# Hymba decoder layer on one core: per-row-block norm and block sums in the second feed-forward, residual in DRAM between the output-projection halves, one weight pool, five plain openers

## The chip, the cores and the metric

The kernel runs on one NeuronCore of a Trainium2 chip. TensorE (PE) multiplies matrices into PSUM; VectorE (DVE), ScalarE (ACT) and GpSimd (POOL) work on tiles in SBUF; SyncE (SP) issues most of the DMA transfers and POOL issues some. Each engine carries out its own list of instructions in order and waits on semaphores of the others. The metric is the device time of one launch in microseconds, lower is better.

## What is computed

One decoder layer on 1024 tokens of width 1024 with 16 meta tokens in front: a half-weighted SwiGLU feed-forward, a mixer of two head groups with an output projection, and a second half-weighted SwiGLU feed-forward, each behind an RMS norm and with a residual.

```python
h = h + 0.5 * swiglu(rms_norm(h, ffn1_norm[l]), ffn1_w_in[l], ffn1_w_out[l])
u = rms_norm(h, mix_norm[l]) @ w_in[l]
...
o_hg = hgrn2(hq, hf, hi, hg, lb_all[l], hgrn_out_norm[l], valid)
o_sb = stick_breaking(sq, sk, sv, sb_q_norm[l], sb_k_norm[l], valid)
o = jnp.concatenate([o_hg, o_sb], axis=-1).astype(h.dtype)
h = h + o @ w_out[l]
h = h + 0.5 * swiglu(rms_norm(h, ffn2_norm[l]), ffn2_w_in[l], ffn2_w_out[l])
```

swiglu(h) is (silu(h @ w_gate) * (h @ w_up)) @ w_out with a hidden width of 2816. Everything is float32.

## The kernel before

**Products in three matmuls.** Each float32 operand is split in two float32r halves: ACT casts to a high half ("wh", "xh", "th", lines 147, 221, 252, 270, 510), then DVE subtracts it to leave a low half ("wl", "xl", "tl", lines 149, 222, 253, 272, 512). A product is three matmuls, high by high, low by high, high by low. So each block of weights or activations costs PE nothing until ACT and DVE have split it.

**Feed-forwards by a seven-product scheme.** The feed-forward matrices are cut two by two and multiplied with seven products in place of eight (Strassen-Winograd): the data blocks B11, B21, B12, B22 give the operands B11, B21, T2, T3, T1, T4, B22, where T2, T3, T1 and T4 are sums of blocks. POOL forms the sums of weight blocks (line 285), DVE those of the data. `fast_in` (from line 257) does the input side: for each pair of column blocks f, one `quad` for the gate and one for the up half. A `quad` takes seven weight operands in turn, 12 matmuls each; PSUM banks a, b and c hold partial sums, which DVE adds up (lines 355, 411, 420). `wp` holds three rotating buffers each for wh, wl and for POOL's sums s, and `in_bufs` buffers for raw weights as they arrive.

The first feed-forward handles 272 of its 1040 rows plainly and 2 x 384 rows by the scheme. Its first four column pairs are "openers": their plain parts (`plain_quad`, four operands each for gate and up, 12 matmuls of 272 columns for each operand) run ahead of everything else, while the remaining rows are loaded, normed (`norm_rows`), transposed on PE eight at a time (`turned`, `first_block`) and combined (`first_combined`, 20 pieces of one cast and one or more subtractions). Each call of `next(steps)` runs one `plain_quad`; four pieces stand between two of them. For later pairs the plain part shares the operands of the quad (`also`), with one more operand; for openers the quad runs alone.

The second feed-forward (n = 512, all rows by the scheme) has two pairs as openers: of their four quads, the B11 and B21 products run first, as the T operands are not there yet.

**`fast_out`** (from line 483) does the output side: seven passes of 11 steps q, each with a weight block `left` (raw loads into `ring`, or the kept tiles sk and ak) and an activation block `right` from DRAM; `between(step, q)` is a hook. In the first feed-forward the hook carries the norm of the plain rows (`first_norm`): squares, `inv_rms_rows` in bank x0, `spread_rows` in x1, then four groups of transposes "hb" that all use bank y3.

**Between the feed-forwards** the output projection runs in two halves over k. The first half (`first_half_of_o`, 16 blocks (i, b) of column half i and row block b, 12 matmuls each, "wo<-wh,oT") is woven between the last recurrence steps of the HGRN heads. At the end of each block it loads the residual `res` and DVE writes the sum into hN2, a tile of 32 KB per partition that stays in SBUF. The second half ("wo<-wh,oH", pool `wo2`, its eight weight blocks of w_out split when it starts) adds to hN2 row block by row block; after each row block `normed(b)` writes the row to DRAM (h2N), norms it (`row_norm`, lines 236 to 240), transposes it (line 247) into the tile `whole`, and for b < 4 splits it into B11 and B21. After the last row block `fast_in` starts; `blocks()` (lines 1684 to 1696) then forms the sums with 16 subtractions of 128x512 and splits 20 tiles of 128x512 (`halve`).

**What sets the order.** PE's order is the program's (manual_schedule). On the other engines and on SP the planner puts in order what is ready, by program order or ahead of it inside `high_priority()`. Pools are stacked from the left or the right end of SBUF. A tile placed where an older pool's tiles were waits for the last use of those it overlaps (reuse_waits="tile").

Of the kernel before, what the change touches and what calls it, by code (L numbers as in the profile page):

```python
# [20 lines left out]
P = 128  # L21
D = 1024
# [17 lines left out]
class Block:  # L40
# [214 lines left out]
    def fast_in(self, ops, n, w_in, actD, openers, ev0, open_ev, feed=None, plain=None,  # L255
# [19 lines left out]
        def block(i, h, col):  # L275
            t = wp.tile([P, 4, P], F32, tag="raw", name="raw", bufs=self.in_bufs)
# [119 lines left out]
        def pair(f, opened=None, also=(None, None)):  # L396
# [17 lines left out]
            def up(i, j, ps, plus):  # L414
# [37 lines left out]
        if plain:  # L452
            for f in ahead:
                gate, up = plain_pair(f)
                plain_quad(f * P, gate)
                yield
                plain_quad(D_FF + f * P, up)
                yield
# [23 lines left out]
    def fast_out(self, out_of, n, w_out, actD, load_h, ready, between=lambda a, q: None,  # L482
# [5 lines left out]
        op, ring, pout = self.op, self.ring, self.pout  # L488
        nq = D_FF // 256
        nb = n // P  # L490
        sk = op.tile([P, nq, 512], F32, name="sk")
        ak = op.tile([P, nq, 512], F32, name="ak")
# [24 lines left out]
        def left(step, q):  # L517

            s, a = sk[:, q, :], ak[:, q, :]
# [16 lines left out]
            return raw(0, 1, q) if step == "A12" else raw(1, 1, q)  # L536
# [32 lines left out]
        for bank, a, b, start, (i, j) in steps:  # L569
# [4 lines left out]
            for q in range(nq):  # L574
                wh, wl = halved(left(a, q), "w", 512)
                xh, xl = halved(right((q, b), n), "t", n)
# [42 lines left out]
    def turned(self, rows, n, banks, evict):  # L619
# [3 lines left out]
        for k0 in range(0, KT, len(banks)):  # L623
            ks = range(k0, k0 + len(banks))
            ps = {k: self.pin.tile([P, n], F32, tag="q" + banks[k - k0], name="xps", bufs=2)
                  for k in ks}
# [6 lines left out]
            for k in ks:  # L633
                evict(k, ps[k])

# [17 lines left out]
    def first_plain(self, rows, junk, x):  # L653
# [9 lines left out]
        self.turned(rows, THIRDS[0][1], "ddbbccaa", evict)  # L663

    def first_block(self, ci, rows, pool, name, ops):
# [3 lines left out]
        got = []  # L669
# [8 lines left out]
        self.turned(rows, n, "bcbc", evict)  # L678
        return got
# [536 lines left out]
    def mix_out(self, k0, plan, o, hN, h1N, pool):  # L1216
# [3 lines left out]
        ws = {}  # L1220

        def part(i, b, k, kept):
            if k == 0:
                if i not in ws:
                    ws[i] = self.mix_weights(k0, i)
                kept["o"] = o(b)
                kept["ps"] = self.pproj.tile([P, 512], F32, tag="proj", name="wo")
# [5 lines left out]
            if k == 3:  # L1233
                h = hN[:, b, 512 * i : 512 * i + 512]
                if k0:
# [526 lines left out]
```

## Time and profile before

| | |
|---|---|
| time, median of 3 runs | 2117.18 us (2116.65 to 2118.34) |
| the profiled execution's own time | 2121.03 us |
| its span, first to last instruction | 2119.2 us |
| mean granted TensorE clock | 0.989 |
| DMA | 303.39 MB, mean 143 GB/s |

The profile's page gives busy time by engine. Its other views, asked of the same execution, are used below: the windows view (for each stretch of time the busy time of each engine with its number of instructions, the granted PE clock, the DMA share and rate), the waits view (who waited for whom: total, times, longest), the groups by line (count, busy time and mean duration in ns, then idle time before them), the chain of work that ended last, the timeline, and the DMA issues with their time to landing. In a row of the timeline stand the start, the duration, engine, line, operation, tiles and in brackets the idle time before it with what ended it. Of successive matmuls, the distance of their starts tells the rate, as their durations overlap.

### The profile page before, as it was taken

The page shows a single profiled execution, that of the slowest core. Times are in us where ns is not written, and L with a number is a line of the kernel's source. Part 1 is how long each engine was busy: PE and PEld are TensorE (multiplying, and loading weights), DVE is VectorE, ACT ScalarE, POOL GpSimd, SP SyncE. Part 2 cuts the span into 40 slices and gives each one's busy share as a digit, 9 for nine tenths or more (in the row PEclk, how much of TensorE's full clock was granted, in tenths as well). Part 3 has the DMA queues.
Part 4 walks back from the last instruction along what each step waited for, and adds up shares of the span by engine and source line. Part 5 has one row for each costly group of instructions (what it writes and reads, how often), then busy time and mean ns, then how long its engine had stood idle before and what let it go on. Part 6 is the DMA issues. An engine that isn't in the chain of part 4 may idle for free.

```text
span 2119.2 us, 31494 instructions
## 1 busy us (share of the span) xinstructions
PE 2028.9 (96%) x11249; PEld 1795.3 (85%) x11249; DVE 1373.6 (65%) x2067; ACT 902.8 (43%) x1854; POOL 624.8 (29%) x676
## 2 busy tenths in 40 slices
PE   7999999999999999999999999988899999999999
PEld 6999999999978799988888888866688888878887
DVE  6776545556688832367778686546667667666774
ACT  7533333334555534466666524145233323333443
POOL 2365534542000002253333201001445445440000
PEclk9999999999999999999999999989999999999999
DMA  6643222227865636343544144623233333349563
GB/s 201 190 142 104 97 82 96 98 67 256 280 213 172 207 108 201 128 138 110 136 121 115 65 179 125 179 90 124 83 107 105 97 108 106 99 158 313 189 224 114
DMA packets 280875, 303.39 MB, mean 143 GB/s; under 512 B 23504, under 2 KB 211280, under 8 KB 280720
## 3 DMA queue, kind: packets, MB, share of 16 engines
q1 hardware_dynamic: 264816, 253.48, 38.8%
q0 software_dynamic: 14864, 47.90, 5.9%
q8 instruction: 89, 1.46, 0.3%
q14 instruction: 66, 0.54, 0.1%
q10 hardware_dynamic: 1040, 0.00, 0.0%
HBM read 221.28 MB, written 80.04 MB: 142 GB/s over the span
## 4 chain that ended last, share of the span: by engine, by line
PE 80%; DVE 6%; DMA 2%; ACT 2%; issue 2%; POOL 0%; DVEq 0%; SPq 0%; ACTq 0%; POOLq 0%
PE o L582 15%; PE qb L313 14%; PE qc L313 9%; PE qa L313 9%; PE proj L162 5%; PE proj L164 5%; PE proj L163 5%; PE qd L313 4%; PE wo L1232 4%; PE o L548 3%; PE flip L1051 2%; PE lvl L820 2%; DMA raw<-in_ffn_w_out_dram 1%; DVE keep L1197 1%; PE oacc L1121 1%
## 5 line engine op out<-in xcount | busy, mean ns | idle before, releaser
L313 PE MATMUL qb<-T,wh 128*128 128x384 f32 (+1 forms) x1056 | 320.4, 364 | 5.8 <-DVE u L355 5.8
L272 DVE TENSOR_TENSOR wl<-s,wh 128x512 fp32r<-128x512 f32 x176 | 199.2, 1133 | 98.8 <-ACT wh L270 94.5
L313 PEld LDWEIGHTS qb<-T,wh 128*128 128x128 f32 x1056 | 196.5, 188 | 30.7 <-ACT wh L270 7.8
L313 PE MATMUL qa<-B,wh 128*128 128x384 f32 (+1 forms) x704 | 217.4, 371 | 3.6 <-ACT wh L270 3.6
L582 PE MATMUL o<-wl,th 128*128 128x512 f32 x539 | 210.4, 392 | 4.2 <-DVE wl L512 4.2
L582 PE MATMUL o<-wh,tl 128*128 128x512 f32 x539 | 210.0, 391 | 3.5 <-DVE tl L512 3.5
L582 PE MATMUL o<-wh,th 128*128 128x512 f32 x539 | 210.5, 392 | 0.0
L272 DVE TENSOR_TENSOR wl<-raw,wh 128x512 fp32r<-128x512 f32 x178 | 165.0, 930 | 63.7 <-ACT wh L270 60.3
L270 ACT CAST wh<-s 128x512 fp32r<-128x512 f32 x176 | 109.4, 622 | 225.8 <-PE qb L313 177.1
L162 PE MATMUL proj<-xh,wh 128*128 128x384 f32 (+2 forms) x576 | 205.4, 357 | 0.2 <-ACT xh L252 0.2
L163 PE MATMUL proj<-xh,wl 128*128 128x384 f32 (+2 forms) x576 | 199.6, 346 | 0.0
L164 PE MATMUL proj<-xl,wh 128*128 128x384 f32 (+2 forms) x576 | 199.2, 346 | 0.1
L313 PE MATMUL qb<-T,wl 128*128 128x384 f32 (+1 forms) x528 | 192.7, 365 | 6.6 <-DVE wl L272 6.6
L270 ACT CAST wh<-raw 128x512 fp32r<-128x512 f32 x178 | 109.8, 620 | 204.0 <-PE qc L313 104.9
L510 ACT CAST th<-act 128x512 fp32r<-128x512 f32 (+2 forms) x176 | 96.5, 549 | 190.8 <-PE o L582 140.3
L313 PEld LDWEIGHTS qa<-B,wh 128*128 128x128 f32 x704 | 132.7, 191 | 20.5 <-ACT wh L270 4.1
L512 DVE TENSOR_TENSOR tl<-act,th 128x512 fp32r<-128x512 f32 (+2 forms) x176 | 107.8, 616 | 63.1 <-ACT th L510 62.1
L313 PE MATMUL qd<-X,wh 128*128 128x272 f32 x704 | 146.1, 294 | 1.3 <-DVE X L661 0.9
L285 POOL TENSOR_TENSOR s<-raw 128x512 f32<-128x512 f32 x88 | 119.5, 1358 | 78.7 <-DVE wl L272 69.3
L313 PE MATMUL qa<-B,wl 128*128 128x384 f32 (+1 forms) x352 | 130.9, 372 | 5.0 <-DVE wl L272 5.0
L1197 DVE TENSOR_TENSOR_SCAN keep<-keep 128x144 f32<-128x144 f32 (+6 forms) x112 | 126.9, 1136 | 9.7 <-ACT keep L1193 7.4
L1202 POOL TENSOR_TENSOR sig<-sig,keep 128x144 f32<-128x144 f32 (+3 forms) x64 | 88.2, 1379 | 143.1 <-DVE keep L1197 80.0
(337 smaller groups left out, 4771.7 us busy)
## 6 DMA issues: line engine op xcount, KB each, us to landing
raw<-in_ffn_w_in_dram SPq DMA_DIRECT2D x216, 256.0 KB, 2.9
raw<-in_ffn_w_out_dram SPq DMA_DIRECT2D x176, 256.0 KB, 4.3
raw<-in_w_in_dram SPq DMA_DIRECT2D x28, 512.0 KB, 4.3
ks<-kD SPq DMA_DIRECT2D x32, 260.0 KB, 5.4
oT<-oD SPq DMA_DIRECT2D x32, 256.0 KB, 3.8
ak<-in_ffn_w_out_dram SPq DMA_DIRECT2D x22, 256.0 KB, 5.0
v<-vD SPq DMA_DIRECT2D x8, 576.0 KB, 4.7
vD<-vhl SPq DMA_DIRECT2D x8, 512.0 KB, 3.7
```

The costliest lines, as they stand in the source:

```text
L162: nc.tensor.matmul(ps, wh[:, s], xs, start=k == 0, stop=False)
L163: nc.tensor.matmul(ps, wl[:, s], xs, start=False, stop=False)
L164: nc.tensor.matmul(ps, wh[:, s], xl[:, k, c0 : c0 + n], start=False, stop=k == nk - 1)
L270: nc.scalar.copy(hi, src)
L272: nc.vector.tensor_sub(lo, src, hi.bitcast(F32))
L285: op(t, x, y)
L313: nc.tensor.matmul(ps, a[:, k, :], b[:, k0 + k, :], start=start and k == 0 and i == 0, stop=k == 3 and i == 2, skip_group_check=True,)
L510: nc.scalar.copy(hi, src)
L512: nc.vector.tensor_sub(lo, src, hi.bitcast(F32))
L582: nc.tensor.matmul(banks[bank][m], z[:, m * P : (m + 1) * P], y, start=start and q == 0 and e == 0, stop=q == nq - 1 and e == 2, skip_grou ...
L1197: nc.vector.tensor_tensor_scan(out=kv, data0=kv, data1=kv, initial=1.0 if last else keep[:, end : end + 1], op0=ALU.mult, op1=ALU.bypass,)
L1202: nc.gpsimd.tensor_mul(sig, sig, keep[:, 1 : nk + 1])
```

## The change

- First feed-forward: five openers in place of four. `plain_quad` yields after each operand, and `turned` after each group of two transposed blocks, so that operands stand between groups of two, and one between two pieces of `first_combined`.
- `first_norm`: banks x3 and y3 in place of x0 and x1, one more step before and after `inv_rms_rows`, and the "hb" groups alternate between y3 and x3.
- Output projection: the residual is loaded into `res` when a block begins (three buffers), the sum is written over it, and POOL's queue stores it to DRAM (hmN). The second half loads rows of hmN into three 4 KB buffers "h". One pool `wo` with eight buffers for each half serves both: the first four blocks of the second half are split three quarters into the first, the next four when it ends. The second half begins with (0,0), (0,1), (1,0), (1,1).
- Second feed-forward: for row blocks 4 to 7, `normed` makes the four subtractions itself; the splits of T2, T3, T1, T4 and B22 go by row block, T2 and T3 of the first three right after the first step of `fast_in`. Raw weights get a pool of their own at the right (`wraw`), opened before the second half of the projection; the openers' loads and splits have high priority; `wq` now lies lowest at the left.
- From `fast_in` to `fast_out`: the last pair's `combined` (four POOL subtractions with their stores) is traced after step q = 2 of the first pass; the loads and splits of steps 0 and 1 have high priority; `ring` moves to the left, and sk and ak are placed at the second pass, after the right-hand pools close.

```diff
@@ weights, plain_quad, up
-                yield operand(block(0, 0, col))
-                yield operand(block(0, 1, col))
+                for h in range(2):
+                    with self.tc.high_priority():
+                        x = operand(block(0, h, col))
+                    yield x
...
                     ps = alone(ps, operand(block(i, h, col)), h, h == 0)
-                take(i, ps)
+                    if h == 1:
+                        take(i, ps)
+                    yield
...
+                elif self.late is None or f // 2 < D_FF // 256 - 1:
+                    combined()
                 else:
-                    combined()
+                    self.late.append(combined)
@@ fast_out
+                with ExitStack() as first:
+                    if a == "A12" and q < 2 and not plain:
+                        first.enter_context(self.tc.high_priority())
+                    wh, wl = halved(left(a, q), "w", 512)
+                    xh, xl = halved(right((q, b), n), "t", n)
@@ first_block, run
-        self.turned(rows, n, "bcbc", evict)
+        yield from self.turned(rows, n, ["bb", "cc", "aa", "bb"], evict)
...
-                        ops, nw, a["ffn1_w_in"][0], act1D, 4, ev0, open_ev, None, plain, between
+                        ops, nw, a["ffn1_w_in"][0], act1D, 5, ev0, open_ev, None, plain, between
...
-                    ba = self.first_block(2, rows[1], rp, "ba", ops)
-                    next(steps)
+                    ba, bb = [], []
+                    for _ in self.first_block(2, rows[1], rp, "ba", ops, ba):
+                        next(steps)
...
-                    for _ in range(5):
-                        for _ in range(4):
-                            next(made, None)
+                    for _ in self.first_combined(ba, bb, ops, rp, nw):
                         next(steps)
@@ output projection
+                    self.weights("wo", 2, 8, c1)
+                    hb = self.pool("hb", ctx=c1)
...
+                    def begin_half(i, b):
+                        t = h[i, b] = mix.tile([P, 512], F32, tag="res", name="res", bufs=3)
+                        nc.sync.dma_start(t, h1N[b, :, cols(i)])
+
+                    def end_half(i, b, ps):
+                        t = h.pop((i, b))
+                        nc.vector.tensor_add(t, ps, t)
+                        nc.gpsimd.dma_start(hmN[b, :, cols(i)], t)
...
+                            if at == 47:
+                                ws[0] = self.mix_weights(0, 0)
...
+                    def begin(i, b):
+                        if b not in h:
+                            h[b] = hb.tile([P, D], F32, tag="h", name="hm", bufs=3)
+                            nc.sync.dma_start(h[b], hmN[b])
...
+                    for b in range(2):
+                        begin(0, b)
+                    ws[1] = self.mix_weights(0, 1)
...
+                    self.wraw = self.pool("wraw", ctx=right, side="right")
@@ normed
+                        if b >= 4:
+                            sub = nc.vector.tensor_sub
+                            c = slice(b * P - n, b * P - n + P)
+                            b11, b21 = (whole[:, 4 * q : 4 * q + 4, c] for q in range(2))
+                            sub(b11, f[0], b11)
+                            sub(t2[:, :, c], f[1], b11)
+                            sub(f[0], f[1], f[0])
+                            sub(b21, b21, t2[:, :, c])
@@ second feed-forward
                 next(steps)
+                for o in ("T2", "T3"):
+                    halves(o, range(3))
                 next(turns[KT - 1])
                 next(steps)
-                next(made)
+                for o in ("T2", "T3"):
+                    halves(o, range(3, 4))
                 next(steps)
-                next(made)
+                halves("T1", range(4))
                 next(steps)
-                drain(made)
+                halves("T4", range(4))
+                halves("B22", range(4))
                 drain(steps)
...
+                    def between(step, q):
+                        if step == "A12" and q == 2:
+                            self.late.pop()()
+                            right.close()
```

More of the change, by code (lines that the diff above doesn't have):

```diff
@@ L454, in fast_in @@
                 gate, up = plain_pair(f)
[L455 to L458, printed above, removed]
+                yield from plain_quad(f * P, gate)
+                yield from plain_quad(D_FF + f * P, up)
             ev["p"] = open_ev()
@@ L535, in left @@
                 return a
-            return raw(0, 1, q) if step == "A12" else raw(1, 1, q)
+            return raw(1, 1, q)
         def plain_round():
```

200 lines of the change are left out of this document (97 added, 103 removed).

## The prediction

> **What bounds the kernel now.** I read the page's busy times first, then the chain, then the windows view over stretches that I chose from PE's waits.
>
> ```profile
> PE 2028.9 (96%) x11249; PEld 1795.3 (85%) x11249; DVE 1373.6 (65%) x2067; ACT 902.8 (43%) x1854; POOL 624.8 (29%) x676
> 498.69 66.45 PE o L548 x525
> 1326.60 2.79 PE wo L1232 x12
> 1602.31 2.72 PE qc L313 x12
> 30.00:62.00 32.00, 24.05 (x165) 21.47 (x164) 27.59 (x64) 31.06 (x65) 2.83 (x6) 0.95 0.39 101
> 1380.00:1404.00 24.00, 15.74 (x35) 8.77 (x35) 7.52 (x11) 6.64 (x12) 2.75 (x3) 0.64 0.36 111
> 1404.00:1448.00 44.00, 43.61 (x218) 35.79 (x216) 23.66 (x36) 19.94 (x40) 3.23 (x6) 1.00 0.20 83
> 1448.00:1500.00 52.00, 36.23 (x129) 27.30 (x130) 36.40 (x54) 24.56 (x44) 10.82 (x9) 0.84 0.37 111
> 1900.00:1912.00 12.00, 8.41 (x26) 5.61 (x25) 11.56 (x13) 2.28 (x4) 7.13 (x7) 0.86 0.99 359
> ```
>
> PE is busy 96% of the span, and the change takes no matmul away. So all that it can win is time in which PE waits, or runs slowly after a wait. The three chain rows give PE's pace when nothing holds it: 0.127 us for a matmul of 272 columns (66.45 / 525), 0.233 for the projection's 512 columns (2.79 / 12), 0.227 for a feed-forward's 512 (2.72 / 12). In a row of the windows view stand the stretch, its length, then PE, PEld, DVE, ACT and POOL with counts, the granted clock, DMA share and GB/s. What each stretch loses is its length less its count at that pace:
>
> - 1380 to 1404, start of the second projection half: 24.0 - 35 x 0.233 = **15.8 us lost**, at a clock of 0.64.
> - 1448 to 1500, start of the second feed-forward: eight of the 129 are transposes (about 1.0 us together, row below), so 52.0 - 121 x 0.227 - 1.0 = **23.5 lost**, at 0.84.
> - 1900 to 1912, from `fast_in` to `fast_out`: 12.0 - 26 x 0.227 = **6.1 lost**, at 0.86.
> - 30 to 62, the openers: 117 matmuls and 48 transposes, 32.0 - 117 x 0.127 - 48 x 0.125 = **11.1 lost**, with ACT busy 31.06 of 32.
>
> ```profile
> L247 PE MATMUL turn<-ident,xn 128*128 128x128 f32 x8 | 1.0, 272 | 0.0
> L313 PE MATMUL qd<-X,wh 128*128 128x272 f32 x78 | 16.1, 299 | 0.4 <-ACT wh L270 0.4
> L313 PE MATMUL qd<-X,wl 128*128 128x272 f32 x39 | 11.7, 300 | 3.8 <-DVE wl L272 3.8
> L629 PE MATMUL xps<-ident,row 128*128 128x128 f32 x48 | 8.4, 312 | 3.8 <-ACT ba L673 2.1 <-ACT bb L673 1.1
> PE wo L1232 <- ACT wh L147: 7.1, 4, 3.1
> PE wo L1232 <- DVE wl L149: 1.2, 2, 1.0
> PE qb L313 <- DVE wl L272: 6.6, 1, 6.6
> PE qa L313 <- DVE wl L272: 5.0, 1, 5.0
> PE qa L313 <- ACT wh L270: 3.6, 1, 3.6
> PE qb L313 <- DVE u L355: 0.9, 1, 0.9
> PE hb L1449 <- ACT hbs L1453: 1.2, 1, 1.2
> PE spread L198 <- DVE inv_rms L185: 1.2, 1, 1.2
> ```
>
> The waits explain about two thirds: 8.3 us of 15.8, and 16.1 of 23.5. The rest is the clock: after a wait of some 3 us PE runs at half pace for a few us.
>
> **The change, part by part.** The sum is made against the profiled execution (2121.03 us); that one stands 3.9 us over the median of 2117.18, and I take the difference off the median.
>
> *Weights of the second half.* PE waited 8.3 us for eight blocks loaded two at a time when the half began. Four of them are now split during the first half, the other four when their buffers come free, at the end of it. PE has two blocks of 2.79 us before it needs those.
>
> ```profile
> raw<-in_w_out_dram SPq DMA_DIRECT2D x8, 256.0 KB, 2.9
> raw<-in_ffn_w_in_dram SPq DMA_DIRECT2D x10, 256.0 KB, 5.3
> 1383.11 0.62 ACT L147 CAST wh<-raw 128x512 fp32r<-128x512 f32 x1 [2.85 <-DMA raw<-in_w_out_dram]
> 1383.76 0.69 DVE L149 TENSOR_TENSOR wl<-raw,wh 128x512 fp32r<-128x512 f32 x1 [2.35 <-ACT wh L147]
> ```
>
> With two raw buffers the third block's load starts some 1.3 us in (0.62 + 0.69), lands at 4.2 and is split at 5.5; it is due at 5.6 + 1.4 = 7.0. The fourth follows 1.3 later and is due 0.7 later. Nearly covered; behind the residual's and the openers' loads a landing can be 5.3 instead of 2.9, which makes it 1 to 2 us late. I leave 2.3 us: **gain 13.5** (bounds 8 and 15.8). The splits that move into the first half lie beside its woven matmuls; without that cover they would cost 4 x 1.3.
>
> *Residual through DRAM.* It adds 16 stores of 256 KB on POOL's queue and 8 loads of 512 KB on SP's; the additions on DVE are as many as before.
>
> ```profile
> res<-h1N SPq DMA_DIRECT2D x16, 256.0 KB, 3.5
> h2N<-hN POOLq DMA_DIRECT2D x8, 512.0 KB, 2.9
> h1N<-hN POOLq DMA_DIRECT2D x6, 512.0 KB, 6.2
> hN<-in_x_dram SPq DMA_DIRECT2D x6, 512.0 KB, 10.0
> 1331.17 2.80 PE wo L1232 x12
> ```
>
> A `res` buffer is now held until its store lands. Blocks start 4.57 us apart (1326.60, 1331.17), three buffers give 13.7 us from end to end. After a block ends: an addition like the 0.69 above, some 0.6 for the issue (an estimate), a store of 2.9 to 6.2, a load of 3.5: 7.7 to 11.0. It fits, cost 0. What waits behind a late `res` load on SP are the `oT` loads of the next block, and PE for those.
>
> *Norm and sums.* In 1404 to 1448 DVE is busy 23.7 of 44 us, so 3.6 us of a row block of 24 x 0.233 + 1.0 = 6.6 us. Row blocks 4 to 7 trade two splits for four subtractions, each some 0.69: 1.4 us more, 5.0 of 6.6. The cover is there, but the subtractions are queued on DVE ahead of the next row's reciprocal and scaling, which PE's transposes wait for: **loss 1**, bounds 0 and 4 (one of 0.69 late in each of four rows, or more).
>
> *Start of the second feed-forward.* The first operands' buffers now lie where the first half of oH was, free halfway, and the raw weights load earlier: the 3.6 us wait and its slow restart go. The 5.0 wait goes by priority. What is late next is DVE's queue ahead of the first T2 product.
>
> ```profile
> L222 DVE TENSOR_TENSOR T<-whole,T 128x512 fp32r<-128x512 f32 x12 | 8.8, 770 | 0.0
> L1684 DVE TENSOR_TENSOR whole<-whole 128x512 f32<-128x512 f32 x4 | 2.7, 686 | 2.4 <-ACT whole L1645 2.4
> 1491.32 1.89 DVE L272 TENSOR_TENSOR wl<-s,wh 128x512 fp32r<-128x512 f32 x3
> ```
>
> DVE does 36.4 us of work in that stretch, nearly all of it before the split of the weight sum (1491.32) that the T2 product takes. Eight of the 16 subtractions (5.4) and three of the eight opener splits (2.1) now fall before the stretch; with the last two wl (1.3) after it, 27.6 us stand before T2. PE has eight products of 2.72 and the transposes, 22.8 us. So PE waits some 4.8, and loses perhaps 2 more to the clock and 0.9 to the wait for "u", which stays: 7.7 of 23.5 remain: **gain 16** (bounds 10 and 22).
>
> *From `fast_in` to `fast_out`.*
>
> ```profile
> 1883.05 0.34 SPq L500 DMA_DIRECT2D raw<-in_ffn_w_out_dram  x1
> 1903.62 3.43 DVE L512 TENSOR_TENSOR tl<-act,th 128x512 fp32r<-128x512 f32 x1
> 1904.01 1.27 POOL L436 TENSOR_TENSOR t<-sg,t 128x512 f32<-128x512 f32 x1
> 1907.11 0.50 PE L582 MATMUL o<-wh,tl 128*128 128x512 f32 x1 [2.86 <-DVE tl L512]
> 1909.37 0.63 PE L582 MATMUL o<-wh,th 128*128 128x512 f32 x1
> 1909.80 0.63 PE L582 MATMUL o<-wl,th 128*128 128x512 f32 x1
> ```
>
> DVE's split of step 1 took 3.43 us while POOL subtracted, PE waited 2.86 us, and then its matmuls start 0.43 apart (1909.37, 1909.80). Splitting steps 0 and 1 early would end that. But POOL has nothing else to do, so tracing its subtractions later need not make them run later; and `ring`, now lowest at the left, lies over wq's split weights: its first raw block may have to wait for the last product, where it was loaded at 1883.05 before; then a landing of 2.9 and a split of 1.3 are open to view, 4.2 us. Between a gain of 5 and a loss of 4 I take **0**.
>
> The 2.86 us wait was enough to halve PE's pace. The Trainium skill, TensorE: Matmul & The Clock Gate, section "Part 1: The HAM clock gate", says that the clock falls to half after at least one idle window of about 3.4 us. By that rule a wait for T2 cut to 3 us would cost no clock, and the sum would be 2 us better, 2078; the row differs, and I go by the row.
>
> *Openers.* In 30 to 62 ACT is the bound: it split data blocks ahead of the openers' weights. Two transposed blocks with one operand of 12 x 0.127 = 1.5 us between them, and one operand per piece, keep PE at work; the fifth opener puts eight more operands there, which need ACT 0.62 and DVE 0.69 each. Pieces with two subtractions still ask more of DVE than 1.5 us, so I leave 3.6 of 11.1: **gain 7.5** (bounds 3 and 10). Its pair later runs without the shared plain part:
>
> ```profile
> PE qb L313 <- DVE u L355: 2.2, 3, 1.0
> ```
>
> Such pairs account for these waits between 62 and 498 us, 1.0 each: **loss 1**. The six operands more and 2 MB of loads lie beside PE work.
>
> *Banks of `first_norm`.* Both 1.2 us waits go: **gain 2.4** (bounds 1 and 3).
>
> Sum: 13.5 - 1 + 16 + 0 + 7.5 - 1 + 2.4 = 37.4; 2117.2 - 37.4 = **2080 us**.
>
> **The rivals.**
> 1. *Everything fits*: T2 isn't waited for and the boundary gains: 15 + 22 + 5 + 9 + 2 = 53, 2064 us. For it: ACT is busy 24.6 of 52 there, and the planner may put the weight sum's split ahead of the last data splits. Against: before, it did not.
> 2. *DVE becomes the bound between the halves*: norms queue behind subtractions and hold the transposes in each of four row blocks, and T2 is as late as before. Gains of the feed-forward's start fall to 10, rows lose 4, the boundary 4, and the openers gain 5: 2117.2 - (13.5 - 4 + 10 - 4 + 5 - 1 + 2.4) = 2095 us. Against: DVE's 23.7 of 44.
> 3. *Slower*: the residual's round trip through DRAM holds `res`, so SP's queue and PE's `oT`. It decides from a store and a load of 12.4 us together (13.7 - 1.3). If both land like the 10.0 us row, a round takes 21.3, three blocks lose 7.6, 16 blocks 40. The three `h` buffers of the second half turn over the same way, 21.3 against some 16 (2.4 row blocks), which adds 5 for every three of the last five: 9. So 2117.2 - 37.4 + 49 = 2129 us. Against it are 2.9 and 3.5.
> 4. *The change doesn't do what it says*: the planner issues the early loads and splits where it issued them before, as the subtractions and casts are ready no sooner; only banks and openers gain: 2117.2 - (7.5 - 1 + 2.4) = 2108 us, and half of the time not even the openers. Against: the second pool of weights was the wait, and it is gone.
>
> Beside these, the Trainium skill, SBUF — State Buffer, section SBUF: two separate sides, says that POOL and DVE lock one port pair and the loser waits for the whole instruction. By that rule the boundary keeps its 6.1 us wherever `combined` is traced, if POOL starts it at the same moment, and my sum stays 2080; the 3.43 us split agrees.
>
> **How the numbers follow.** Forecast 0.60; rivals 1 0.16, 2 0.12, 3 0.06, 4 0.06. All bad bounds together leave a gain of 8 - 4 + 10 - 4 + 3 - 1 + 1 = 13, 2104 us; the good ones give 2064. With rival 3, 4 and the worst of 2 left out, 2063 to 2100 should hold 8 in 10. A measurement of this kernel tells some 0.2%, 4.2 us, from no change. Faster by more: the forecast, 1, 2 and half of 4: 0.91; within it: the other half of 4 and 0.01 of 3: 0.04; slower by more: the rest of 3: 0.05.
>
> **What would show it.** In the changed trace: no wait of "wo" for wh; a granted clock near 1.0 where it was 0.64; the first T2 product 25 to 30 us after the last projection matmul, waiting for DVE's wl; the "hb" and "spread" waits gone; 30 to 62 with fewer waits for ACT. The forecast is wrong if `oT` or `h` loads appear as PE's releasers, or if PE waits for the first raw block of `fast_out`.

## The result and the profile after

| | before | changed |
|---|---|---|
| median | 2116.91 us (2115.77 to 2118.34, 4 runs) | 2095.98 us (2094.4 to 2098.1, 4 runs) |
| profiled execution, its span | 2121.03, 2119.2 us | 2094.55, 2092.8 us |
| mean granted clock | 0.989 | 0.993 |
| DMA | 303.39 MB | 313.90 MB |

The ratio of the changed kernel's time to the time before is 0.9901 (95%: 0.9884 to 0.9919): 1% faster, 20.9 us between the medians. Forecast were 2080 us and a gain of 37.4; the time lies in the range of 2063 to 2100, and the gain is 56% of the forecast one.

The windows view of the changed kernel over the same stages (columns as in the prediction). The projection's second half now begins at 1375.8 and the second feed-forward at 1428.4.

```profile
30.00:62.00 32.00, 27.01 (x201) 26.41 (x199) 23.37 (x52) 27.37 (x54) 2.22 (x5) 0.89 0.45 117
1376.00:1400.00 24.00, 22.64 (x106) 18.09 (x105) 13.99 (x21) 9.58 (x19) 4.44 (x6) 1.00 0.67 216
1400.00:1428.00 28.00, 27.88 (x144) 23.15 (x142) 18.97 (x30) 13.18 (x27) 2.13 (x4) 1.00 0.38 145
1428.00:1480.00 52.00, 46.45 (x199) 36.40 (x200) 40.33 (x58) 29.32 (x53) 16.66 (x14) 1.00 0.36 102
1860.00:1900.00 40.00, 30.27 (x109) 23.84 (x108) 20.07 (x27) 14.02 (x24) 7.85 (x9) 0.83 0.95 363
```

The same view for the transposes alone (xps in the first stretch, turn in the others) and, from the kernel before, for 40 us around its boundary of `fast_in` and `fast_out`:

```profile
30.00:62.00 32.00, 5.85 (x44) 4.84 (x42) 0.00 (x0) 8.45 (x16) 0.89 0.45 117
...
1376.00:1400.00 24.00, 2.16 (x16) 1.71 (x16) 0.00 (x0) 2.22 (x4) 1.00 0.67 216
...
1428.00:1480.00 52.00, 1.04 (x8) 0.94 (x8) 0.00 (x0) 1.07 (x2) 1.00 0.36 102
```

```profile
1896.00:1936.00 40.00, 36.41 (x150) 28.75 (x149) 25.98 (x35) 13.79 (x24) 8.55 (x10) 0.96 0.96 353
```

And the waits of PE in the changed kernel, in 62 to 500, 560 to 740 and 1220 to 1380:

```profile
PE qb L315 <- DVE u L359: 3.1, 3, 1.1
PE qc L315 <- DVE wl L272: 1.4, 1, 1.4
PE qd L315 <- DVE wl L272: 0.6, 1, 0.6
...
PE o L593 <- DVE wl L515: 0.9, 1, 0.9
PE o L593 <- DVE tl L515: 0.7, 1, 0.7
...
PE wo L1244 <- DMA oT<-oD: 4.1, 2, 3.7
```

Counted as in the prediction (length less count at PE's pace), the stages lose, in us:

| stage | before | after | gain | forecast |
|---|---|---|---|---|
| 30 to 62, openers | 11.1 | 32 - 157 x 0.127 - 44 x 0.125 = 6.6 | 4.5 | 7.5 |
| 62 to 500, waits alone | 3.6 | 5.1 | -1.5 | -1 |
| 560 to 740, waits alone | 6.5 | 1.6 | 4.9 | 2.4 |
| end of the first projection half, oT | 0 | 4.1, with slow matmuls behind it 5.5 | -5.5 | 0 |
| second half, first 24 us | 15.8 | 24 - 90 x 0.233 - 16 x 0.125 = 1.0 | 14.8 | 13.5 - 1 |
| start of the second feed-forward | 23.5 | 52 - 191 x 0.227 - 1.0 = 7.6 | 15.9 | 16 |
| `fast_in` to `fast_out`, 40 us | 40 - 150 x 0.227 = 6.0 | 40 - 109 x 0.227 = 15.3 | -9.3 | 0 |

The gains add up to 23.8 of the 26.5 us between the two profiled executions. These lie further apart than the medians (20.9 us): the one before stands 4.1 us above its median, the changed one 1.4 below. The middle of the kernel gave what was forecast and some more: no wait for the projection's weights is left, the rows of 1400 to 1428 (144 matmuls, 40 of them transposes) lose nothing at this pace, and the clock is 1.00 where it was 0.64 and 0.84. The shortfall lies where the forecast said 0: 15 us at two places. At the boundary the changed kernel's timeline shows this (SP, ACT, DVE, POOL and PE in this order):

```profile
1862.25 0.84 SPq L503 DMA_DIRECT2D raw<-in_ffn_w_out_dram  x2
...
1866.03 6.14 SPq L1772 DMA_DIRECT2D hN<-h2N  x8
1874.13 0.33 SPq L503 DMA_DIRECT2D raw<-in_ffn_w_out_dram  x1
...
1864.94 0.62 ACT L513 CAST wh<-raw 128x512 fp32r<-128x512 f32 x1 [10.17 <-DMA raw<-in_ffn_w_out_dram]
1867.86 1.27 ACT L513 CAST th<-act 128x512 fp32r<-128x512 f32 x2 [1.37 <-DMA act<-act0B]
...
1865.59 3.93 DVE L515 TENSOR_TENSOR wl<-raw,wh 128x512 fp32r<-128x512 f32 x2 [1.92 <-ACT wh L513]
...
1863.76 1.25 POOL L442 TENSOR_TENSOR t<-sg 128x512 f32<-128x512 f32 x1 [1.96 <-DVE sg L425]
...
1861.83 0.39 PE L315 MATMUL qc<-B,wh 128*128 128x512 f32 x1
1868.53 2.07 PE L593 MATMUL o<-wh,th 128*128 128x512 f32 x4 [6.32 <-ACT th L513]
...
1885.74 0.80 PE L593 MATMUL o<-wh,th 128*128 128x512 f32 x1 [3.42 <-ACT th L513]
```

SP's first raw loads of `fast_out` go out at 1862.25, 0.4 us after the last matmul of `fast_in` begins; in the kernel before, the first went out at 1883.05 (the prediction's row), and `fast_out` began at 1899.3. PE waits 6.32 us for the cast of the first act block, which landed last. Four steps later it waits again, 3.42 us: the raw block of step 4 was issued at 1874.13, behind eight loads of h, 4 MB. POOL's first late subtraction starts right behind DVE's last sg, as it did before.

### The profile page after: what moved, and what is told of

Same layout as the page of the kernel before. It is cut to its first block, busy times and chain, and to the rows that moved or that the text cites. A ratio compares the mean times of both kernels' runs of the same rounds, so it can differ in the third digit from the quotient of the medians.

```text
span 2092.8 us, 31593 instructions
## 1 busy us (share of the span) xinstructions
PE 2013.8 (96%) x11249; PEld 1788.4 (85%) x11249; DVE 1380.0 (66%) x2073; ACT 903.9 (43%) x1859; POOL 632.2 (30%) x692
## 2 busy tenths in 40 slices
DMA packets 287534, 313.90 MB, mean 150 GB/s; under 512 B 24016, under 2 KB 215888, under 8 KB 287376
## 4 chain that ended last, share of the span: by engine, by line
PE 77%; DVE 5%; ACT 2%; DMA 2%; issue 2%; POOL 0%; SPq 0%; DVEq 0%; ACTq 0%; POOLq 0%
PE o L593 17%; PE qb L315 13%; PE qc L315 8%; PE qa L315 8%; PE proj L164 5%; PE proj L162 5%; PE proj L163 5%; PE qd L315 3%; PE o L556 3%; PE wo L1244 3%; PE flip L1063 2%; PE lvl L832 2%; DVE keep L1209 1%; PE oacc L1133 1%; PE oacc L1135 1%
## 5 line engine op out<-in xcount | busy, mean ns | idle before, releaser
L272 DVE TENSOR_TENSOR wl<-raw,wh 128x512 fp32r<-128x512 f32 x184 | 172.2, 938 | 53.6 <-ACT wh L270 49.9
```

The lines of the kernel that those rows point to most:

```text
L272: nc.vector.tensor_sub(lo, src, hi.bitcast(F32))
```

## The experiments

Twelve kernels, each the changed one with the edits named. Their ratios are to the kernel before, and the last column is (ratio - 0.9901) x 2117; each ratio is good to about 0.0015 (3 us), so differences under some 5 us are read from the stage and not from the time.

| run | median us | ratio (95%) | us against the changed kernel |
|---|---|---|---|
| h3 first | 2091.12 | 0.9869 (0.9854 to 0.9883) | -7 |
| h loads later | 2089.03 | 0.9864 (0.9849 to 0.9879) | -8 |
| POOL's sums not late | 2094.04 | 0.9891 (0.9876 to 0.9907) | -2 |
| h3 in tiles, h later | 2088.49 | 0.9860 (0.9844 to 0.9876) | -9 |
| oT before res | 2096.0 | 0.9891 (0.9874 to 0.9907) | -2 |
| six res buffers | 2092.57 | 0.9879 (0.9864 to 0.9894) | -5 |
| hm loads behind oT | 2091.31 | 0.9877 (0.9860 to 0.9893) | -5 |
| weights traced late | 2095.52 | 0.9890 (0.9876 to 0.9905) | -2 |
| sums traced late | 2096.28 | 0.9909 (0.9894 to 0.9924) | +2 |
| sums over all row blocks | 2105.18 | 0.9946 (0.9930 to 0.9963) | +10 |
| four openers, old banks | 2100.91 | 0.9931 (0.9914 to 0.9947) | +6 |
| three mends together | 2077.82 | 0.9819 (0.9804 to 0.9833) | -17 |

### The boundary: where ring lies, when h is loaded, who subtracts

```diff
+                    hN = self.pool("h3", ctx=c1).tile([P, KT, D], F32, name="hN3")
                     self.ring = self.pool("ring", ctx=c1)
...
-                    hN = self.pool("h3", ctx=c1).tile([P, KT, D], F32, name="hN3")
```

> The changed kernel with one edit: the pool h3 of the second fast_out is opened ahead of ring and parts, so that ring no longer lies over the weight buffers wq. Theory (ring waits for the last product of fast_in): the raw loads start some 15 us before the end of fast_in instead of 0.4 us after the last product begins; the 6.32 us wait of PE for th goes, and the 3.42 us one some 13 us later shrinks; 9 to 13 us less than the changed kernel's 2096, so 2083 to 2087. Rival (POOL's late subtractions slow DVE's splits, as in the kernel before, and the loads are not what counts): the first loads come early, but PE still waits some 3 us for tl or th; 2090 to 2093. Third case (the 4 MB of h loads block SP's queue): the 6.32 wait goes, the 3.42 one stays; 2087 to 2090.

Its window over 40 us, and its timeline:

```profile
1854.00:1894.00 40.00, 34.95 (x140) 27.51 (x139) 23.26 (x30) 14.97 (x26) 8.64 (x10) 0.91 0.98 364
```

```profile
1862.51 1.21 PE L593 MATMUL o<-wl,th 128*128 128x512 f32 x4 [1.21 <-DVE wl L515]
...
1864.08 4.04 DVE L515 TENSOR_TENSOR tl<-act,th 128x512 fp32r<-128x512 f32 x2
...
1864.47 1.27 POOL L442 TENSOR_TENSOR t<-sg,t 128x512 f32<-128x512 f32 x1
...
1867.57 2.08 PE L593 MATMUL o<-wh,tl 128*128 128x512 f32 x4 [3.85 <-DVE tl L515]
```

40 - 140 x 0.227 = 8.2 us are lost instead of 15.3, and both waits for th are gone. So the place of ring was the cause of some 7 us. Two others stand in their place: PE waits for wl and tl, which DVE splits behind its last sg while POOL subtracts, as in the kernel before. The rival had named what is late next, and its time came true.

```diff
-                if a == "A12" and q == 3 and not plain:
+                if a == "A12" and q == 6 and not plain:
                     load_h()
```

> The changed kernel with one edit: the eight loads of h (512 KB each) of the second fast_out are issued after step q = 6 of the first pass instead of q = 3. Theory (the second wait of 3.42 us comes from raw and act blocks of q = 4 that stand behind 4 MB of h on the queue): the 6.32 us wait stays, the 3.42 us one and its slow restart go; 4 to 6 us less than 2096, so 2090 to 2092. Rival (the second wait is only the ring catching up from its late start, whatever else is loaded): 3 us of wait stay, 2095 to 2097.

```profile
1860.00:1900.00 40.00, 34.29 (x139) 27.07 (x138) 22.73 (x31) 15.78 (x26) 8.76 (x10) 0.91 0.93 353
```

The wait for the first th stays (5.0 us), the second is gone, and 40 - 139 x 0.227 = 8.4 us are lost. The 4 MB of h on SP's queue were the cause of the second wait. Either edit alone, ring moved or h later, gains about 7 us; the two don't add up, as the next run but one shows.

```diff
-                elif self.late is None or f // 2 < D_FF // 256 - 1:
+                else:
                     combined()
-                else:
-                    self.late.append(combined)
```

> The changed kernel with one edit: the last pair's four subtractions on POOL are traced where the kernel before had them, not after step q = 2 of fast_out. Theory (POOL runs them at the same moment either way, as it has nothing else to do): no change, 2094 to 2098, POOL's subtractions start within 0.5 us of the same place against the last product. Rival (tracing them late is worth something, or costs something, as their stores move on POOL's queue): 3 us or more of difference.

PE waits 6.1 and 4.5 us for th, and 40 us lose 40 - 117 x 0.227 = 13.4. Tracing the subtractions late was worth nothing that these runs can show: POOL runs them when they are ready.

```diff
+                    h3 = self.pool("h3", ctx=c1)
+                    hN = [h3.tile([P, D], F32, name=f"hN3{b}") for b in range(5)]
                     self.ring = self.pool("ring", ctx=c1)
...
+                    hN += [hN2.tile([P, D], F32, name=f"hN3{b}") for hN2 in (self.pool("h3b", ctx=c1),)
+                           for b in range(5, KT)]
```

(and the h loads after q = 6, as above)

> The changed kernel with the tile hN3 of the second fast_out as eight tiles of 4 KB, five of them below ring and three above parts, so that the first buffers of ring and of the split weights lie over operands (T2, T3, T1) that are done three products or more before the end, and with the h loads after step q = 6. With h3 wholly below ring, parts still lay over T4 and B22, the first tl waited for the last product, and PE waited 1.2 us for wl and 3.8 us for tl while POOL subtracted. Theory (both splits and loads were late by their places in SBUF): steps 0 and 1 are split before the last product ends, POOL's subtractions hide behind them, the stretch from 1860 loses 1 to 3 us instead of 15.6; 2082 to 2085. Rival (the planner puts the splits behind the last u and sg on DVE whatever their place): wl and tl are still waited for, 2087 to 2091.

PE still waits 1.2 us for wl and 3.9 for tl, and 8.0 us are lost (141 matmuls in 40 us). ACT's casts for steps 0 and 1 were done by 1861.2, and they write into the same pool, so its buffers were very likely free. But the splits stand behind the last u and sg on DVE all the same (from 1864.88), where they meet POOL's subtractions; the two of tl take 5.76 us. The rival held.

### The oT wait at the end of the first projection half

```diff
-                begin(i, b)
                 kept["ps"] = self.pproj.tile([P, 512], F32, tag="proj", name="wo")
                 kept["o"] = o(b)
+                begin(i, b)
```

> The changed kernel with one edit: in mix_out the load of oT is issued ahead of begin, so ahead of the load of res, for each block. Theory (a res load waits on SP for the store of the block three before, and the oT loads stand behind it): PE's waits for oT (4.1 us between 1354 and 1363) go, 4 to 6 us less than 2096, so 2090 to 2092. Rival (the DMA engines are full there with the loads of hm, of the second half's weights and KB, and oT lands late whatever its place): the waits stay within 1.5 us of what they are, 2095 to 2097.

One wait of 3.2 us for oT stays: the rival held.

```diff
-                        t = h[i, b] = mix.tile([P, 512], F32, tag="res", name="res", bufs=3)
+                        t = h[i, b] = mix.tile([P, 512], F32, tag="res", name="res", bufs=6)
```

> The changed kernel with one edit: six buffers for res in place of three. Theory (a res load at the head of SP's queue waits for the store of the block that held its buffer, 26.1 us in ten waits between 1318 and 1372, and the oT loads stand behind it): with six buffers a load needs the store of six blocks before, SP no longer waits, oT is issued some 9 us sooner; PE's wait for oT (2.2 to 4.1 us in the runs so far, 5 us with its slow restart) goes, 2090 to 2093. Rival (the DMA engines are full there, 80% over 22 us, with the loads of hm, KB and the weights, and oT lands late whatever SP does): 2 us or more of wait for oT stay, 2095 to 2097.

Again the rival's wait stays: PE waits 2.2 us for oT, though SP waits less for the stores (18.2 us in seven waits, not 26.1 in ten). The time lies in the theory's range, but that doesn't speak for the buffers: runs that left this stage alone wait for oT between 2.2 us (h3 first) and 3.8 us (sums traced late).

```diff
-                    for b in range(2):
-                        begin(0, b)
+                    with tc.issue_after(self.last_oT.ins):
+                        for b in range(2):
+                            begin(0, b)
```

(`self.last_oT` is the last load that `from_dram` issued)

> The changed kernel with one edit: the first two loads of hm (512 KB each) for the second projection half are queued on SP behind the last oT load of the first half. Theory (full DMA engines): the wait for oT near 1360 shrinks below 1 us, 2091 to 2094. Rival (SP held by res): the wait for oT stays at 2 us or more, 2095 to 2098; and if hm then comes late for the end of the second half's first block, DVE waits for it and nothing else does.

Here no wait for oT is left, though SP waits 25.8 us for the stores of hmN, as long as ever. The DMA issues in 1340 to 1362, with KB each and the median time to landing, of the changed kernel, of the run with six res buffers, and of this one:

```profile
oT<-oD SPq DMA_DIRECT2D x8, 256.0 KB, 7.0
hm<-hmN SPq DMA_DIRECT2D x3, 512.0 KB, 7.5
```

```profile
oT<-oD SPq DMA_DIRECT2D x9, 256.0 KB, 7.1
hm<-hmN SPq DMA_DIRECT2D x3, 512.0 KB, 8.1
```

```profile
oT<-oD SPq DMA_DIRECT2D x10, 256.0 KB, 4.8
```

So what holds PE is not the `res` buffer but 1.5 MB of hm, which the planner issues while the first half still runs, because the rows are complete. An oT load lands after 7.0 us beside them and after 4.8 without them. The hm loads move to 1364 to 1368, and nothing waits for them there.

### The second half and the start of the feed-forward

```diff
-                            if at == 47:
-                                ws[0] = self.mix_weights(0, 0)
...
-                    ws[1] = self.mix_weights(0, 1)
+                    ws.update((i, self.mix_weights(0, i)) for i in range(2))
```

> The changed kernel with one edit: all eight weight blocks of the second projection half are traced when it begins, none after step 47 of the first. Theory (the early tracing is what wins, as in the term of 13.5 us): PE waits for wh and wl again at the start of the half, the clock falls, 8 to 12 us more than 2096, 2104 to 2108. Rival (the one pool is what wins: its buffers come free as the blocks of the first column half are done, and loads and splits are issued then wherever they are traced): 2094 to 2098, no wait for wh.

PE waits for no weight in the second half and the time is unchanged. The planner issues the loads when buffers come free, wherever they are traced: the first goes out at 1334.89, in the changed kernel at 1333.80, in the kernel before, which had a second pool for them, at 1380.05. So the early loads make the gain, and what lets them be early is, by elimination, the common pool. No run undid the pool, nor the new order of the first four blocks, which gives PE work that needs only the first four weights.

```diff
-                        if b >= 4:
+                        for b in range(4, KT) if b == KT - 1 else ():
...
+                            f = [whole[:, 4 * q : 4 * q + 4, c] for q in range(2)]
```

> The changed kernel with one edit: all sixteen subtractions of the second feed-forward's data blocks are traced after the last row block, with the splits of T2 and T3 behind them, as in the kernel before; pools, weights and priorities stay as changed. Forecast's theory (DVE's queue ahead of the first T2 product is what is late): eight subtractions (5.4 us) and some splits fall between the last row and T2, PE waits 5 to 7 us for wl more, the stretch 1448 to 1500 loses 6 to 9 us more: 2102 to 2106. Rival (pools and priorities were the wait, and the planner hides the sums anyway): 2095 to 2098.

```profile
1420.02 0.69 DVE L1696 TENSOR_TENSOR whole<-whole 128x512 f32<-128x512 f32 x1 [1.35 <-ACT whole L1685]
```

Traced together after the last row, the subtractions of the first three row blocks still run right behind each row (from 1420.02, 1426.38 and 1432.71), as each needs only its own row block. The run undid next to nothing, so it says nothing about the sums themselves. The next one does:

```diff
+                def halves(o):
+                    for j in range(4):
...
+                        if o == "T2":
+                            sub(b11, b12, b11)
+                            sub(t2[:, j], b22, b11)
...
+                        self.halve(ops[o], floats[o][:, j], j)
```

> The changed kernel with one edit: the sixteen subtractions and the splits of T2, T3, T1, T4 and B22 go over all four row blocks at once (128 x 512 of one k), as in the kernel before, in place of by row block; pools, weights and priorities stay as changed. With the row-block sums only traced later the planner still ran them right behind each row, so that run did not undo them; this one does, as a sum needs the last row block. Theory (the granularity by row block is what shortens DVE's queue ahead of the first T2 product): eight subtractions and four splits, some 8 us of DVE, fall between the last row block and T2; PE waits 5 to 9 us for wl where it waits 1.3 now, the clock falls, 1448 to 1510 loses 7 to 12 us more: 2103 to 2108. Rival (the place of the buffers and the early weights were the whole gain there): under 2 us more, 2095 to 2098.

Its waits and its window:

```profile
PE qb L315 <- DVE wl L272: 9.6, 1, 9.6
```

```profile
1427.00:1479.00 52.00, 38.63 (x156) 29.67 (x157) 39.85 (x59) 26.74 (x48) 11.80 (x10) 0.90 0.32 91
```

52 - 148 x 0.227 - 1.0 = 17.4 us lost, 9.8 more than with sums by row block, and the time is 9 to 10 us longer. Of the 15.9 us gained at the start of the second feed-forward, the row-block form is worth about 10; the other 6 stay with what was not undone, the pools and the priorities; no run parts these.

### Openers and banks

```diff
-                        ops, nw, a["ffn1_w_in"][0], act1D, 5, ev0, open_ev, None, plain, between
+                        ops, nw, a["ffn1_w_in"][0], act1D, 4, ev0, open_ev, None, plain, between
...
-                    for _ in self.first_combined(ba, bb, ops, rp, nw):
-                        next(steps)
+                    for at, _ in enumerate(self.first_combined(ba, bb, ops, rp, nw)):
+                        if at % 5 < 3:
+                            next(steps)
...
-                        r = self.inv_rms_rows(acc, n, pn, self.pout, "x3")
+                        r = self.inv_rms_rows(acc, n, pn, self.pout, "x0")
```

(and x1 for y3 in `spread_rows`, y3 for all four hb groups)

> The changed kernel with two edits in two stretches. (1) Four openers in place of five, with the change's fine order (an operand between two pieces in 12 of 20 places). Theory (the fifth opener's eight operands are cover for the data pieces, as in the term of 7.5 us): 30 to 62 loses 2 to 5 us more, and 62 to 500 loses about 1 less. Rival (ACT is the bound there, and eight operands more only add work to it): the same loss or less. (2) first_norm with banks x0, x1 and y3 as in the kernel before: the waits for hbs and inv_rms (1.2 each) come back between 577 and 720, 2.4 us by the forecast, up to 6 if the clock or the splits behind it suffer too. Together 2098 to 2104; if the openers lose nothing, 2095 to 2099.

In 30 to 62 the same is lost as with five (32 - 153 x 0.127 - 44 x 0.125 = 7.1), and PE waits the same 4.8 us for wh. The loss comes later, when the openers are used up before the data pieces are done. POOL's first weight sums then run beside DVE's splits:

```profile
74.78 2.16 POOL L285 TENSOR_TENSOR s<-raw 128x512 f32<-128x512 f32 x1 [4.78 <-DMA raw<-in_ffn_w_in_dram]
...
78.82 1.75 DVE L272 TENSOR_TENSOR wl<-raw,wh 128x512 fp32r<-128x512 f32 x1
...
80.62 0.59 PE L315 MATMUL qd<-X,wl 128*128 128x272 f32 x1 [3.98 <-DVE wl L272]
```

The waits in 62 to 500 add up to 8.1 us instead of 5.1, and a slow restart follows the longest. So the fifth opener is worth some 5 us (3.0 of waits, 0.5 in 30 to 62 and the slow restart; the time is 6 us longer), but not in the stage where the forecast put it. The banks by themselves are worth almost nothing: the hb wait comes back as 0.2 us, none for inv_rms. What took those two waits away is then probably the steps that were added around `inv_rms_rows`, which stayed in; that was not tried alone.

### Three mends together

```diff
-                sub = nc.gpsimd.tensor_sub
+                sub = (nc.gpsimd if self.late is None or f // 2 < D_FF // 256 - 1
+                       else nc.vector).tensor_sub
...
-                            self.late.pop()()
+                            with tc.issue_after(self.lo.ins):
+                                self.late.pop()()
...
-                    ps = alone(ps, operand(block(i, h, col)), h, h == 0)
+                    t = block(i, h, col)
+                    with self.tc.high_priority():
+                        x = operand(t)
+                    ps = alone(ps, x, h, h == 0)
```

(with the tiles of hN3, the later h loads and the hm loads behind oT, as above; `self.lo` is the last subtraction of `halved`)

> The changed kernel with four edits that touch three stretches, each to be read in its own. (1) 1840 to 1900: hN3 in tiles of 4 KB below ring and above parts, the h loads after step q = 6, and the last pair's four subtractions on DVE in place of POOL, queued behind the split of step 2. Theory (the 8.4 us that are still lost there once the loads are early are DVE's splits under POOL's subtractions): wl and tl of step 0 take 0.7 each again, PE waits 2 us or less in all, the stretch loses 2 to 4 us instead of 15.6. Rival (PE waits because the splits stand behind the last u and sg, whoever subtracts): 6 us or more stay. (2) 1340 to 1380: hm loads behind the last oT load: no wait for oT, as with that edit alone. (3) 30 to 62: the cast and the subtraction of each opener's operand have high priority. Theory (PE's wait of 4.86 us for wh comes from ACT's own bursts ahead of the operands' casts): 3 to 5 us less lost there. Rival (the raw blocks arrive late, so that no priority helps, or the data splits are late in their place and hold PE's transposes): the same loss as before, 8 us in 30 to 62, or more. All together, 2072 to 2080.

```profile
30.00:62.00 32.00, 28.88 (x231) 28.45 (x232) 25.52 (x57) 31.53 (x64) 3.15 (x6) 1.00 0.51 132
1850.00:1890.00 40.00, 37.28 (x161) 29.54 (x161) 24.18 (x39) 15.88 (x28) 3.26 (x6) 1.00 0.96 348
```

```profile
1858.62 1.28 DVE L519 TENSOR_TENSOR wl<-raw,wh 128x512 fp32r<-128x512 f32 x2
...
1859.35 1.21 PE L597 MATMUL o<-wl,th 128*128 128x512 f32 x4 [1.21 <-DVE wl L519]
...
1859.82 1.28 DVE L519 TENSOR_TENSOR tl<-act,th 128x512 fp32r<-128x512 f32 x2
```

All three theories held, but for one bound: PE waits 1.2 and 1.5 us at the boundary, 2.7 in all where at most 2 were expected. Two splits take 1.28 us there, not 4.04 (h3 first) or 5.76 (h3 in tiles), once POOL does not subtract beside them; the clock stays at 1.00, and 3.5 us are lost instead of 15.3. No wait for oT is left. In 30 to 62, with 46 transposes among the 231, 2.8 us are lost instead of 6.6. The three stages give 11.8, 5.5 and 3.8 us, 21.1 together, against 18.2 us between the medians. The kernel takes 2077.82 us: 0.9819 of the time before, faster than both.

## Why the prediction was right, and where it was not

The time lies inside the range, but not because the sum was right: two terms taken as 0 lost 14.8 us, and the range was wide enough to hold that. It is also, within 1 us, the time of rival 2 (2095), but that is chance: rival 2 had four rows late and T2 as late as before, while no row lost and the wait for T2's weights was 1.3 us.

**Right: the middle.** The second half's weights gained 14.8 us (13.5 forecast) and the rows behind it lost nothing (1 forecast); the start of the second feed-forward gained 15.9 (16 forecast). The reason given for the start of the feed-forward, DVE's queue ahead of the first T2 product, is shown by the run with sums over all row blocks: PE waits 9.6 us for exactly that wl. The wait that was left came out smaller than the 4.8 us forecast, while more stayed elsewhere; first its row, then two other waits of PE in 1428 to 1480:

```profile
1456.36 0.51 PE L315 MATMUL qb<-T,wl 128*128 128x512 f32 x1 [1.33 <-DVE wl L272]
```

```profile
PE qb L315 <- DVE u L359: 1.8, 2, 0.9
PE qa L315 <- DVE sg L421: 1.4, 1, 1.4
```

With 0.9 for the B operands and 0.2 more for sg the waits make 5.6 of the 7.6 us that are left; the other 2.0 is not traced to a wait, and the clock was 1.00. So the remainder (7.7 forecast) is right in sum and not in its parts: that agreement is partly luck. In the second half of the projection, tracing the weights early was not what made them early; the pool is the likely reason.

**Wrong: the boundary as 0, bounds -5 to 4; it lost 9.3.** The mechanism was named (ring lies over the last product's buffers, 4.2 us), and so was the one that would not help (tracing POOL's sums late). The step failed in its size and in what comes after. The landing was taken as 2.9 us, but raw and act blocks leave together and the first th is cast 6.0 us after the last matmul of `fast_in` begins (1861.83 to 1867.86). And the queue behind was left out: a ring that starts late has four steps loaded when 4 MB of h join the same queue, which costs a second wait of 3.42 us and its slow restart.

**Wrong: the residual as 0; it lost 5.5.** The sum of the round trip was right (between 1318 and 1372 a store landed in 4.2 us and a load in 3.2, medians), SP was held by `res` as described, and that is not what PE waits for: neither six buffers nor another order took the wait away. The term counted the hm loads as part of the second half. The planner issues them in the first, beside the oT loads, and those land 2.2 us later for it (7.0 against 4.8). Rival 3 had named the right wait, PE's for `oT`, but the wrong cause.

**Too large: the openers, 4.5 where 7.5 was forecast.** Two transposed blocks with an operand between them don't keep PE at work when ACT takes the evictions and splits first. The changed kernel's timeline of ACT, and PE's wait:

```profile
37.56 1.07 ACT L686 ACTIVATE ba<-xps,g 128x384 f32<-128x384 f32 x2
38.50 0.94 ACT L221 CAST B<-ba 128x384 fp32r<-128x384 f32 x2
...
39.76 1.28 ACT L661 ACT_TABLE_LOAD   x1
...
41.26 1.04 ACT L660 ACTIVATE junk<-row 128x1024 bf16<-128x1024 f32 x1
...
42.30 0.60 ACT L270 CAST wh<-raw 128x512 fp32r<-128x512 f32 x1
...
42.95 0.60 PE L315 MATMUL qd<-X,wh 128*128 128x272 f32 x1 [4.86 <-ACT wh L270]
```

Evictions, splits, a table load and the next rows' squares all stand ahead of the cast that PE waits for. With priority for these casts the stage loses 2.8 instead of 11.1: a gain of 8.3, inside the bounds of 3 and 10.

**Banks, 2.4 forecast:** both named waits went, but only 0.2 us of them came back with the old banks; the added steps are the likely reason. The rest of the 4.9 there is waits for wl (3.4 before, 0.9 after), and these vary between kernels that are alike in this stage: 2.9 in the run with three mends.

Both signs that the prediction named for its being wrong appeared: oT loads as PE's releaser, and a wait for the first blocks of `fast_out` (of the two, the act block came last). Of its signs for being right one did not come: between 30 and 62 PE waits for ACT once in place of four times, but 4.9 us in place of 3.6.

Three readings in its working are off, none by enough to change the forecast. The waits explain 53% of the 15.8 us and 69% of the 23.5, not two thirds of each. The good bounds add up to 15.8 + 22 + 5 + 10 - 1 + 3 = 54.8 us, which is 2062 us and not 2064. And the three waits for u are 0.7 us each on average; 1.0 is the longest.

The Trainium skill, SBUF — State Buffer, section SBUF: two separate sides, says that a VectorE instruction with two inputs in SBUF and a GpSimd instruction that reads SBUF need one shared port pair, and that whichever starts later is blocked for the other's whole instruction. The runs agree: with POOL subtracting beside them (1.27 us each), two splits took 4.04 us, without it 1.28.

## What to carry to other kernels

When a pool moves, list what its first buffers lie over and when that is last used, and then walk the queue on for several steps: a late start meets the next large load. A planner that issues what is ready makes the place of a line in the program a poor guide; what counts is when buffers and data come free, so order that must hold has to be forced, for loads that come too early as well as for those that come too late. A large load that is ready early is not free: it delays the small ones beside it (here 7.0 us to landing against 4.8).

## What was not expected of the hardware

How long PE may wait before it slows down has no sharp bound in these runs. The first matmuls after a wait for oT, in the run with h3 first and in the one with six res buffers:

```profile
1357.76 1.22 PE L1244 MATMUL wo<-wh,oT 128*128 128x512 f32 x2 [2.17 <-DMA oT<-oD]
1358.78 0.63 PE L1244 MATMUL wo<-wl,oT 128*128 128x512 f32 x1
```

```profile
1359.49 0.73 PE L1244 MATMUL wo<-wh,oT 128*128 128x512 f32 x2 [2.22 <-DMA oT<-oD]
1360.06 0.39 PE L1244 MATMUL wo<-wl,oT 128*128 128x512 f32 x1
```

After 2.17 us two matmuls take 1.02 us from start to start of the next, half pace; after 2.22 us they take 0.57. A wait of 2.25 us (h loads later) was followed by half pace and one of 2.51 (POOL's sums not late) was not. In the kernel before, after the wait of 2.86 us, four matmuls still started at full pace, and half pace set in 1.0 us after the wait (1907.11 to 1908.14). Behind the waits of 3.42 us and more in the changed kernel, half pace lasted 3 to 5 us. The Trainium skill, TensorE: Matmul & The Clock Gate, section "Part 1: The HAM clock gate", gives at least one idle window of about 3.4 us for the fall; here waits of 2.17 and 2.25 us were enough.
